# Weight sums for Winograd products made by accumulating DMAs, and six more pairs that use them

## The chip, the cores and the metric

The kernel runs on one core of a Trainium2 chip. The metric is the device time of one execution in microseconds, as the median of several runs. The engines are called as the profile calls them: PE (TensorE, matrix multiplications), PEld (its weight loads), DVE (VectorE, elementwise), ACT (ScalarE, activations and casts), POOL (GpSimd, here almost only an issuer of DMAs) and SP (SyncE, an issuer of DMAs). All DMAs run on the core's 16 DMA engines.

## The reference

Two layers, 256 positions, width 2048, float32. Layer 0 mixes with a gated MLP, layer 1 with latent attention, and each is followed by a convolutional feed-forward part. The change concerns the mixer of layer 0:

```python
def gmlp_mixer(x, w_in, ln_g, ln_b, w_s, b_s, w_out):
    z = jax.nn.gelu(x @ w_in)                  # w_in: 2048 x 12288
    u, v = jnp.split(z, 2, axis=-1)
    v = layer_norm(v, ln_g, ln_b)
    ...
    s = jnp.einsum('gij,bnjgd->bnigd', w, v) + ...
    return (u * s.reshape(B, S, GM_HALF)) @ w_out      # w_out: 6144 x 2048
```

`x @ w_in` is called the input projection here (first its V half, then its U half), the last line the output projection, also called spatial projection.

## The kernel before, in words

**Products.** The operands are float32. Each is split into a high part that TensorE takes in its faster float32 form and a low rest; a product of blocks is then three matmuls, high by high, low by high and high by low, each with 512 columns. The weights come in pieces of 1 MB, a "pair": two blocks of 128 rows (k) by 1024 columns, that is four quarters of 128 x 512. With the two halves of the 256 positions, a pair takes eight block products, 24 matmuls ("wide", `Banks.eight`). A "seven" pair (`Banks.seven`) uses Winograd's form of the 2 x 2 product: seven block products, 21 matmuls, for which sums of the quarters of the weights are needed, and sums and differences of the activations.

**Feed.** `Feed` streams the pairs in the order of use. `_load` issues the DMA of a pair from SP into one of three `raw` buffers. `_split` makes the parts: ACT casts the high part (`wh`, line 125), DVE subtracts for the low part (`wl`, line 128). For a seven pair `_seven` first makes the sums on DVE (`ts`, line 135: one addition of 1024 columns and two of 512), and casts and subtracts them too (`th`, `tl`). These parts lie in 14 buffers with the tag `big`, which are also used by activations. `next` runs two splits and two more loads ahead of use. In the feed-forward parts some pairs are "parked": made ahead in idle time, stored in DRAM and fetched by POOL; that stays as it is.

**Stages.** The V half of the input projection has six groups of eight pairs (until about 255 us), the U half six groups (until about 535 us), the output projection two halves of 24 pairs, in the order of the table `PLAN`: a number is the pair of k blocks, the letter its kind (e wide, s seven, p parked). The activations of a pair are made by `Acts.make`, in another form for a seven pair.

**Rows for the norm.** In the U half each group normalizes a part of v on DVE (`norm_v`, lines 831 and 832) with rows that POOL fetches by DMA (`row_v`, line 808, tiles `vr`). The first of these fetches stands right after the V half; the matmuls of `spatial` need the normalized v, and they stand third in the first U group.

**Order.** Each engine executes its instructions in the order of the program. An instruction that waits for a semaphore holds up all behind it on its engine. POOL and SP too: a DMA that waits stands in front of those behind it. `behind` places a DMA's issue in that order behind the latest matmul; it makes no wait.

Of the kernel before, what the change touches and what calls it, by code (L numbers as in the profile page):

```python
# [66 lines left out]
KEEP = {"wide": 4, "seven": 6, "parked": 6}  # L69


def plan(n_k):
# [4 lines left out]
class Feed:  # L77
# [3 lines left out]
    def __init__(self, nc, pin, behind, order, pool, dram, chunks):  # L81
        self.pin, self.behind, self.order, self.sums = pin, behind, order, None
        self.nc, self.pool, self.dram, self.chunks = nc, pool, dram, chunks
        self.kept = {}
        self.raw, self.parts = {}, {}
        self.loaded = self.split = self.used = 0

    def _load(self):
        ap, cols, kind = self.chunks[self.loaded][:3]
        if kind == "parked":  # L90
            self.fetch(self.loaded)
            self.loaded += 1
            return
        t = self.pool.tile([P, 2048], F32, tag="raw", name=f"raw{self.loaded}", bufs=SLOTS["raw"])
        if len(ap.shape) == 3:
            self.behind(self.nc.sync.dma_start(t.rearrange("p (k c) -> p k c", k=ap.shape[1]), ap))
        else:
            step = 1024 if self.loaded < 3 else cols
            for o in range(0, cols, step):
                self.behind(self.nc.sync.dma_start(t[:, o : o + step], ap[:, o : o + step]))  # L100
        self.raw[self.loaded] = t
        self.loaded += 1

    def _split(self):
        i = self.split
        cols, kind = self.chunks[i][1:3]
        if kind == "parked":
            self.split += 1
# [12 lines left out]
        self.parts[i] = (hi, lo)  # L121
        self.split += 1
# [8 lines left out]
    def _seven(self, i, raw):  # L131
# [78 lines left out]
def trunk(ctx: ExitStack, tc: tile.TileContext, x, xT, gm_in, gm_wout, ffn_up, ffn_dn,  # L210
# [30 lines left out]
            order(ins, recent[0])  # L241


    chunks, parked = [], []
    n_up = ffn_up.shape[1]
    for g in range(6):
        for p in V_PAIRS[g]:
# [7 lines left out]
    def back(w, n_k):  # L255

        for hf, units in enumerate(plan(n_k)):
            c = slice(hf * 1024, (hf + 1) * 1024)
            for u, kind in units:
                if 2 * u + 1 == n_k:  # L260
                    chunks.append((w[2 * u, :, c], 1024, kind))
                    continue
                if kind == "parked":
                    parked.append(len(chunks))
                chunks.append((w[2 * u : 2 * u + 2, :, c].rearrange("k p c -> p k c"), 2048, kind))

    back(gm_wout, NF_GM)
# [137 lines left out]
    class Banks:  # L405
# [29 lines left out]
        def seven(self, a, sums, wh, wl, th, tl, turned=0, across=False):  # L435
# [4 lines left out]
            self.to("q4", a[1][1], th, tl, 1536)  # L440
            self.to("q5", s1, th, tl, turned)
            self.to("p7", s3, th, tl, 512 - turned)
            self.to("p6", s2, th, tl, 1024)

        def rest(self):

# [46 lines left out]
    def down(n_k, src, tag, ln, acts, skew=SKEW, tiles=None, beside=None):  # L493
# [6 lines left out]
        for hf, units in enumerate(seq):  # L500
# [3 lines left out]
            for i, (u, kind) in enumerate(units):  # L504
# [13 lines left out]
                elif kind == "wide":  # L518
                    acc.eight(a, *got)
                else:  # L520
                    acc.seven(a, sums, *got, 512 if kind == "parked" else 0)
# [229 lines left out]
    for gi in range(6):  # L751
# [600 lines left out]
```

## Time and profile before

| | us |
|---|---|
| time, median of 3 runs (2465.39 to 2465.87) | 2465.41 |
| the profiled execution, first to last instruction | 2464.6 |
| PE busy in it | 2458.1 |
| DVE busy | 2054.7 |
| ACT busy | 1459.3 |
| POOL busy | 104.2 |
| share of the time in which the DMA engines move weights for SP's queue | 52.9% |
| the same for POOL's queue | 15.8% |

A matmul's duration in the profile is its passage through the array; the next one starts before it ends, so a stage's pace is read from its busy time over its number of matmuls. Times within the span count from its start. In the views, "[1.76 <-DMA vr<-gbrows]" behind an instruction is the time that its engine sat idle before it, and what ended that; "x40, 1024.0 KB, 4.8" behind a DMA are its count, its size and the median time in us from its issue to its landing.

### The profile page before, as it was taken

How to read it: one execution, taken by the hardware profiler on the slowest of the kernel's cores; microseconds unless marked ns; L12 is line 12 of the kernel's file. 1: busy time of each engine (PE TensorE's matmuls, PEld its weight loads, DVE VectorE, ACT ScalarE, POOL GpSimd, SP SyncE). 2: the span in 40 equal slices, each digit the busy share in tenths (PEclk: the TensorE clock that was granted, in tenths of full speed). 3: DMA queues.
4: the chain of work that ended last, by engine and by line, in shares of the span. 5: the costliest groups of instructions: out<-in, count | busy, mean ns of one | idle time of the engine just before them, and what ended most of it. 6: DMA issues, size and time to landing. Idle time of an engine off the chain costs nothing. (4 is left out here: it accounts for less than half of the span.)

```text
span 2464.6 us, 32483 instructions
## 1 busy us (share of the span) xinstructions
PE 2458.1 (100%) x12494; PEld 2091.3 (85%) x12494; DVE 2054.7 (83%) x2734; ACT 1459.3 (59%) x1967; POOL 104.2 (4%) x202
## 2 busy tenths in 40 slices
PE   9999999999999999999999999999999999999999
PEld 7888888888888888888888888988888888888887
DVE  7999999989897788778777997867598787878798
ACT  6666665566565666656554566665565665555453
POOL 0000000000000000000001000000000000000000
PEclk9999999999999999999999999999999999999999
DMA  7555666656665778778868885544478787777885
GB/s 291 202 208 205 226 204 202 205 188 205 222 212 198 241 282 314 300 279 300 322 218 318 301 301 182 184 170 156 172 269 309 275 305 304 295 265 278 299 324 201
DMA packets 116428, 611.94 MB, mean 248 GB/s; under 512 B 10648, under 2 KB 10912, under 8 KB 75184
## 3 DMA queue, kind: packets, MB, share of 16 engines
q1 hardware_dynamic: 90128, 462.47, 52.9%
q0 software_dynamic: 26144, 147.39, 15.8%
q8 instruction: 98, 1.61, 0.3%
q14 instruction: 58, 0.48, 0.1%
HBM read 544.75 MB, written 65.06 MB: 247 GB/s over the span
## 5 line engine op out<-in xcount | busy, mean ns | idle before, releaser
L128 DVE TENSOR_TENSOR wl<-raw,wh 128x1024 fp32r<-128x1024 f32 (+4 forms) x645 | 958.4, 1501 | 169.5 <-ACT wh L125 124.0
L125 ACT CAST wh<-raw 128x1024 fp32r<-128x1024 f32 (+4 forms) x645 | 809.0, 1278 | 356.8 <-PE up L230 80.7
L230 PE MATMUL up<-xhl,wh 128*128 128x512 f32 x2624 | 611.4, 390 | 0.0
L230 PEld LDWEIGHTS up<-xhl,wh 128*128 128x128 f32 x2624 | 487.4, 188 | 97.8
L230 PEld LDWEIGHTS up<-xhl,wl 128*128 128x128 f32 x2624 | 325.8, 192 | 6.4
L230 PE MATMUL up<-xhl,wl 128*128 128x256 f32 x2624 | 328.1, 283 | 0.0
L125 ACT CAST th<-ts 128x1536 fp32r<-128x1536 f32 (+1 forms) x138 | 142.5, 1052 | 110.9 <-DVE ts L135 80.3
L230 PE MATMUL ub<-wh,xhl 128*128 128x512 f32 x576 | 179.5, 393 | 0.0
L128 DVE TENSOR_TENSOR tl<-ts,th 128x1536 fp32r<-128x1536 f32 (+1 forms) x138 | 163.2, 1221 | 10.4 <-PE dn_p L230 3.4
L230 PEld LDWEIGHTS ub<-wh,xhl 128*128 128x128 f32 x576 | 108.1, 188 | 24.2 <-issue 1.9
L230 PE MATMUL ub<-wl,xhl 128*128 128x512 f32 x288 | 112.1, 389 | 0.0
L135 DVE TENSOR_TENSOR ts<-ts,raw 128x512 f32<-128x512 f32 x138 | 95.1, 689 | 1.4
L135 DVE TENSOR_TENSOR ts<-raw 128x1024 f32<-128x1024 f32 x69 | 84.3, 1221 | 6.1 <-PE ub L230 3.8
L230 PE MATMUL mo<-wh,oT 128*128 128x512 f32 x256 | 82.5, 401 | 0.0
L230 PE MATMUL v_q<-wh,xhl 128*128 128x512 f32 x224 | 70.7, 391 | 0.3 <-ACT wh L125 0.3
L230 PEld LDWEIGHTS ub<-wl,xhl 128*128 128x128 f32 x288 | 54.1, 188 | 11.3
L230 PE MATMUL v_p<-wh,xhl 128*128 128x512 f32 x192 | 59.9, 389 | 0.0
L230 PEld LDWEIGHTS mo<-wh,oT 128*128 128x128 f32 x256 | 45.5, 189 | 7.1
L230 PEld LDWEIGHTS v_q<-wh,xhl 128*128 128x128 f32 x224 | 42.0, 188 | 10.5 <-ACT wh L125 1.9
L230 PE MATMUL mo<-wl,oT 128*128 128x512 f32 x128 | 50.1, 391 | 0.0
L724 ACT ACTIVATE lny<-lnt,lncol 128x128 f32<-128x128 f32 x96 | 36.6, 472 | 15.6 <-PE lnt L720 15.5
L388 DVE TENSOR_TENSOR h_0a<-up,lo_0a 128x256 f32<-128x256 f32 x41 | 17.2, 421 | 33.0 <-ACT lo_0a L386 33.0
(1838 smaller groups left out, 4338.4 us busy)
## 6 DMA issues: line engine op xcount, KB each, us to landing
raw<-in_ffn_up_dram SPq DMA_DIRECT2D x172, 1024.0 KB, 7.0
raw<-in_gm_in_dram SPq DMA_DIRECT2D x93, 1024.0 KB, 5.3
raw<-in_ffn_dn_dram SPq DMA_DIRECT2D x68, 1024.0 KB, 7.2
raw<-in_gm_wout_dram SPq DMA_DIRECT2D x48, 1024.0 KB, 5.3
praw<-in_ffn_dn_dram POOLq DMA_DIRECT2D x16, 1024.0 KB, 13.9
keptth<-pth POOLq DMA_DIRECT2D x16, 1024.0 KB, 8.1
kepttl<-ptl POOLq DMA_DIRECT2D x16, 1024.0 KB, 8.8
fth<-keptth POOLq DMA_DIRECT2D x16, 1024.0 KB, 9.4
```

Of the source, the lines that this page charges most:

```text
L125: cast = self.nc.scalar.copy(hi, raw)
L128: self.nc.vector.tensor_tensor(lo, raw, hi.bitcast(F32), ALU.subtract)
L135: add = lambda o, a, b: self.nc.vector.tensor_tensor(o, a, b, ALU.add)
L230: recent[0] = nc.tensor.matmul(o, l, r, start=start, stop=stop, skip_group_check=True)
L388: nc.vector.tensor_tensor(h, acc[:, 0:S], lo, ALU.add)
L724: nc.scalar.activation(y[:, j], t[:, j * P : (j + 1) * P], AF.Identity, bias=lncol[:, o : o + 1], scale=lncol[:, g : g + 1])
```

## The change

A new kind of pair, "t" (summed), is added. Its four sums aren't made on DVE from the raw quarters, but ahead of time in DRAM, by `give`: POOL issues a DMA that writes the first quarter r0 four times into a DRAM buffer `given` (r0 r0 r0 r0), and three accumulating DMAs that add r1 to the first three, r2 to the last three, and r3 to the third. Source and target both lie in DRAM. `sums_ahead` takes the fourteen pairs two at a time, one step of both at each call, and is called after every second pair of V groups 1 to 5 (20 steps) and of the U groups until it is through (8 more). In the output projection a summed pair is loaded by three DMAs of SP: the quarters r1, r2, r3 into `raw` (r0 isn't used alone), and the sums into a `big` buffer. The table for the output projection has 14 "t" and 5 "s" pairs, where there were 13 "s"; the program has 18 matmuls fewer.

```diff
-PLAN = {NF_GM: ("0e 1e 2s 3e 4e 5s 6e 7e 8s 9e 10e 11s 12e 13e 14s 15e 16e 17s 18e 19e 20s 21e 22e 23e",
-                "23e 22e 21e 20s 19e 18e 17s 16e 15e 14s 13e 12e 11s 10e 9e 8s 7e 6e 5s 4e 3e 2e 1e 0e"),
+PLAN = {NF_GM: ("0e 1e 2s 3e 4t 5e 6e 7t 8e 9e 10t 11e 12t 13e 14t 15e 16t 17e 18t 19e 20s 21e 22e 23e",
+                "23e 22e 21e 20s 19e 18t 17e 16t 15e 14t 13e 12t 11e 10t 9e 8s 7t 6e 5s 4t 3e 2e 1e 0e"),
...
-KINDS = {"e": "wide", "s": "seven", "p": "parked"}
+KINDS = {"e": "wide", "s": "seven", "p": "parked", "t": "summed"}
...
 def _load(self):
...
-        if len(ap.shape) == 3:
+        if kind == "summed":
+            d = self.given.pop(self.loaded)
+            s = self.pool.tile([P, 2048], F32, tag="big", name=f"ts{self.loaded}", bufs=SLOTS["big"])
+            self.behind(self.nc.sync.dma_start(t[:, 512:1024], ap[:, 0, 512:1024]))
+            self.behind(self.nc.sync.dma_start(t[:, 1024:2048], ap[:, 1]))
+            self.behind(self.nc.sync.dma_start(s, d))
+            t = (t, s)
+        elif len(ap.shape) == 3:
...
 def _split(self):
...
+        if kind == "summed":
+            big = lambda n: self.pool.tile([P, 2048], F32R, tag="big", name=f"{n}{i}", bufs=SLOTS["big"])
+            wh, wl, th, tl = [big(n) for n in ("wh", "wl", "th", "tl")]
+            self._cast(wh[:, 0:1536], wl[:, 0:1536], raw[0][:, 512:2048])
+            self._cast(th, tl, raw[1])
+            self.parts[i] = (wh, wl, th, tl)
+            self.split += 1
+            return
...
+    def give(self, i):
+
+        ap, pin = self.chunks[i][0], self.pin
+        d = self.dram.tile([P, 2048], F32, tag=f"given{i}", name=f"given{i}", bufs=1)
+        self.given[i] = d
+        o = d.rearrange("p (n c) -> p n c", n=4)
+        r = lambda k, f, n: ap[:, k : k + 1, f * 512 : f * 512 + 512].to_broadcast([P, n, 512])
+        for n, (t, x) in enumerate(((o, r(0, 0, 4)), (o[:, 0:3], r(0, 1, 3)), (o[:, 1:4], r(1, 0, 3)), (o[:, 2:3], r(1, 1, 1)))):
+            ins = self.nc.gpsimd.dma_start(t, x) if n == 0 else self.nc.gpsimd.dma_start(t, x, accum_op=ALU.add)
+            self.behind(pin(ins))
+            yield
...
+    def sums_ahead():
+
+        for i, j in zip(summed[::2], summed[1::2]):
+            for _ in zip(feed.give(i), feed.give(j)):
+                yield
+
+    ahead = sums_ahead()
...
             got = feed.next()
+            if gi and c % 2:
+                next(ahead, None)
...
             got = feed.next()
+            if c % 2:
+                next(ahead, None)
```

How this stands in POOL's order, first at the start of the V groups. `wT` are the spatial weights, a `given` number is one pair's buffer, DMASW counters count landings of POOL's own DMAs. Before, the row fetches (`vr`) follow the last of `wT`:

```order
L781 DMA wT_1978<-in_w_sT_dram 128x256 [waits DMAHW6_49,PE_49]
L782 MEMSET wT_1969 64x2x64 [waits DMASW0_49,Pool_49]
L782 MEMSET wT_1972 64x2x64 [waits DMASW2_49]
L782 MEMSET wT_1975 64x2x64 [waits DMASW3_49]
L782 MEMSET wT_1978 64x2x64 [waits DMASW4_49]
L808 DMA vr_1998<-gbrows 128x512 [waits DMASW1_49,DVE_49,Activation_49]
L808 DMA vr_2000<-gbrows 128x512 [waits DVE_49,Activation_49]
```

Now the first two pairs follow there:

```order
L171 DMA given_526<-in_gm_wout_dram 512x1x512
L171 DMA given_528<-in_gm_wout_dram 512x1x512
L822 MEMSET wT_2022 64x2x64 [waits DMASW2_49]
L822 MEMSET wT_2025 64x2x64 [waits DMASW3_49]
L822 MEMSET wT_2028 64x2x64 [waits DMASW4_49]
L171 DMA given_526<-in_gm_wout_dram 128x3x512 [waits DMASW5_49]
L171 DMA given_528<-in_gm_wout_dram 128x3x512 [waits DMASW6_49]
L171 DMA given_526<-in_gm_wout_dram 128x3x512 [waits DMASW7_49,DMASW1_49]
L171 DMA given_528<-in_gm_wout_dram 128x3x512 [waits DMASW0_49]
L171 DMA given_526<-in_gm_wout_dram 128x512 [waits DMASW1_49]
L171 DMA given_528<-in_gm_wout_dram 128x512 [waits DMASW2_49]
```

Forty such DMAs, ten pairs, stand ahead of the first row fetch, and none waits for another engine. The end of that series, and what follows it:

```order
L171 DMA given_1779<-in_gm_wout_dram 128x3x512 [waits DMASW7_49]
L171 DMA given_1781<-in_gm_wout_dram 128x3x512 [waits DMASW0_49]
L171 DMA given_1779<-in_gm_wout_dram 128x512 [waits DMASW3_49,DMASW1_49]
L171 DMA given_1781<-in_gm_wout_dram 128x512 [waits DMASW4_49,DMASW2_49]
L848 DMA vr_2048<-gbrows 128x512 [waits DVE_49,Activation_49]
L848 DMA vr_2050<-gbrows 128x512 [waits DVE_49,Activation_49]
```

The row fetches of the first U group are now behind the last accumulating steps of the fifth two pairs; the sixth and the seventh two pairs stand ahead of the fetches for the third and the fourth part of v. The compute engines' order in the whole input projection is as it was.

In SP's order at the start of the output projection, before:

```order
L96 DMA raw_3945<-in_gm_wout_dram 128x2x1024 [waits DMAHW7_49,DVE_49]
L96 DMA raw_3999<-in_gm_wout_dram 128x2x1024 [waits DMAHW0_49,DVE_49]
L96 DMA raw_4032<-in_gm_wout_dram 128x2x1024 [waits DMAHW1_49,DVE_49,Activation_49]
L96 DMA raw_4064<-in_gm_wout_dram 128x2x1024 [waits DMAHW2_49,DVE_49]
L96 DMA raw_4131<-in_gm_wout_dram 128x2x1024 [waits DMAHW3_49,DVE_49]
```

and now:

```order
L103 DMA raw_4015<-in_gm_wout_dram 128x2x1024 [waits DMAHW7_49,DVE_49]
L98 DMA raw_4069<-in_gm_wout_dram 128x512 [waits DMAHW0_49,DVE_49]
L99 DMA raw_4069<-in_gm_wout_dram 128x1024
L100 DMA ts_4070<-given_526 128x2048 [waits DMASW5_49,DMASW3_49,DMASW7_49,DMASW1_49,PE_49]
L103 DMA raw_4105<-in_gm_wout_dram 128x2x1024 [waits DMAHW1_49,DVE_49,Activation_49]
```

A load of one pair has become three, and the third waits for TensorE (PE), which frees the buffer, and for the chain of that pair, ahead of the next raw load.

More of the change, by code (lines that the diff above doesn't have):

```diff
@@ L56 @@
 SLOTS = {"big": 14, "raw": 3, "side": 6}
-PLAN = {NF_GM: ("0e 1e 2s 3e 4e 5s 6e 7e 8s 9e 10e 11s 12e 13e 14s 15e 16e 17s 18e 19e 20s 21e 22e 23e",
-                "23e 22e 21e 20s 19e 18e 17s 16e 15e 14s 13e 12e 11s 10e 9e 8s 7e 6e 5s 4e 3e 2e 1e 0e"),
+PLAN = {NF_GM: ("0e 1e 2s 3e 4t 5e 6e 7t 8e 9e 10t 11e 12t 13e 14t 15e 16t 17e 18t 19e 20s 21e 22e 23e",
+                "23e 22e 21e 20s 19e 18t 17e 16t 15e 14t 13e 12t 11e 10t 9e 8s 7t 6e 5s 4t 3e 2e 1e 0e"),
         NF_FF: ("0e 1p 2e 3s 4e 5e 6p 7e 8s 9e 10e 11p 12e 13s 14e 15p 16e 17s 18e 19s 20e 21e",
                 "21e 20e 19p 18e 17s 16e 15p 14e 13s 12e 11p 10s 9e 8s 7p 6e 5s 4e 3e 2e 1e 0e")}
-KINDS = {"e": "wide", "s": "seven", "p": "parked"}
+KINDS = {"e": "wide", "s": "seven", "p": "parked", "t": "summed"}
 FIRST = ((19, 1), (20, 0), (20, 2))
 LEAD = 5
-KEEP = {"wide": 4, "seven": 6, "parked": 6}
+KEEP = {"wide": 4, "seven": 6, "parked": 6, "summed": 6}
 def plan(n_k):
@@ L83, in __init__ @@
         self.nc, self.pool, self.dram, self.chunks = nc, pool, dram, chunks
-        self.kept = {}
+        self.kept, self.given = {}, {}
         self.raw, self.parts = {}, {}
@@ L241, in behind @@
             order(ins, recent[0])
-    chunks, parked = [], []
+    chunks, parked, summed = [], [], []
     n_up = ffn_up.shape[1]
@@ L264, in back @@
                     parked.append(len(chunks))
+                if kind == "summed":
+                    summed.append(len(chunks))
                 chunks.append((w[2 * u : 2 * u + 2, :, c].rearrange("k p c -> p k c"), 2048, kind))
@@ L433, in first, with seven @@
             self.begun.update(DIRECT)
-        def seven(self, a, sums, wh, wl, th, tl, turned=0, across=False):
+        def seven(self, a, sums, wh, wl, th, tl, turned=0, across=False, at=(1536, 1024)):
             s1, s2, s3, s4 = sums
@@ L439, in seven @@
             self.to("p1", a[0][0], wh, wl, 512 if across else 0)
[L440 removed]
+            q4, p6 = at
+            self.to("q4", a[1][1], th, tl, q4)
             self.to("q5", s1, th, tl, turned)
[L442 to L443 removed]
+            self.to("p7", s3, th, tl, 512 - turned if p6 == 1024 else 1536)
+            self.to("p6", s2, th, tl, p6)
         def rest(self):
@@ L520, in down @@
                 else:
-                    acc.seven(a, sums, *got, 512 if kind == "parked" else 0)
+                    acc.seven(a, sums, *got, 512 if kind == "parked" else 0, at=(1024, 512) if kind == "summed" else (1536, 1024))
                     if u == last:
```

## The prediction

> **What bounds the kernel now.** I read the page first: the busy shares say which engine sets the end.
>
> ```profile
> span 2464.6 us, 32483 instructions
> PE 2458.1 (100%) x12494; PEld 2091.3 (85%) x12494; DVE 2054.7 (83%) x2734; ACT 1459.3 (59%) x1967; POOL 104.2 (4%) x202
> ```
>
> TensorE (PE) is never idle, so a matmul that goes is time that goes, and any wait that reaches TensorE is time that comes. The next view is the table of windows, cut where the change works: V part of the input projection from the first possible sum to the first row fetch (57.5 to 253.8 us), the first two groups of its U part, and the output projection (columns: stretch; then busy us and instructions of PE, PEld, DVE, ACT, POOL; clock; share of the 16 DMA engines; GB/s).
>
> ```profile
> 57.50:253.80 196.30, 196.30 (x868) 162.54 (x867) 189.39 (x170) 129.62 (x149) 0.23 (x2) 1.00 0.59 208
> 253.80:302.70 48.90, 48.90 (x214) 39.89 (x213) 44.31 (x58) 29.31 (x40) 4.29 (x9) 1.00 0.68 230
> 302.70:346.90 44.20, 44.20 (x198) 35.50 (x197) 42.83 (x44) 27.20 (x28) 2.12 (x4) 1.00 0.64 211
> 535.00:789.80 254.80, 254.80 (x1137) 211.16 (x1137) 227.76 (x255) 147.65 (x145) 0.72 (x1) 1.00 0.63 211
> ```
>
> Three readings. TensorE starts a matmul every 196.30 / 868 = 0.226 us. VectorE (DVE) is busy 189.39 of 196.30 us in V, 96%, so it can hardly catch up there after a delay. The DMA engines are 59% to 68% busy, always with weights; GpSimd (POOL) has almost nothing to do until 253.8 us. What it does then is in its timeline:
>
> ```profile
> 253.83 0.54 POOL L808 DMA_DIRECT2D vr<-gbrows  x1 [195.98 <-issue]
> 269.55 0.54 POOL L808 DMA_DIRECT2D vr<-gbrows  x1 [2.46 <-DVE vrs L351]
> 302.68 0.54 POOL L808 DMA_DIRECT2D vr<-gbrows  x1 [32.59 <-DVE u0u L453]
> 306.87 1.74 POOL L808 DMA_DIRECT2D vr<-gbrows  x3 [3.65 <-DVE v L896]
> 346.93 0.54 POOL L808 DMA_DIRECT2D vr<-gbrows  x1 [38.32 <-DVE u1u L453]
> ```
>
> It fetches the rows (vr) of the gating unit's norm. The timelines of VectorE and TensorE show who waits for them:
>
> ```profile
> 260.86 0.75 DVE L831 SCALAR_TENSOR_TENSOR v<-v,vmv,vr 128x512 f32<-128x512 f32 x1 [1.76 <-DMA vr<-gbrows]
> 279.87 2.35 DVE L128 TENSOR_TENSOR tl<-ts,th 128x1536 fp32r<-128x1536 f32 x2
> 282.39 0.62 PE L230 MATMUL ub<-th,xhl 128*128 128x512 f32 x2
> ```
>
> VectorE already waits 1.76 us for the first row, and at 282.39 TensorE begins on weights whose low part VectorE finishes at 282.2. There is no reserve at this place: what the rows come late, TensorE waits.
>
> **The change, part by part.** *Matmuls.* Thirteen pairs with 21 products of halves become nineteen (five "s" and fourteen "t" in the new plan; the words of the change say 17). Six pairs lose three matmuls each: 18 x 0.226 = 4.1 us less. This is the whole gain, 0.17% of the time.
>
> *VectorE in the output projection.* Eight pairs fewer are summed there. By the groups of that window, kept apart by shape:
>
> ```profile
> L135 DVE TENSOR_TENSOR ts<-raw 128x1024 f32<-128x1024 f32 x12 | 14.7, 1222 | 4.0 <-PE ub L230 3.4 <-PE wo_q L230 0.7
> L135 DVE TENSOR_TENSOR ts<-ts,raw 128x512 f32<-128x512 f32 x25 | 17.2, 687 | 0.2
> L128 DVE TENSOR_TENSOR tl<-ts,th 128x1536 fp32r<-128x1536 f32 x13 | 22.8, 1753 | 0.2 <-ACT th L125 0.2
> L128 DVE TENSOR_TENSOR wl<-raw,wh 128x2048 fp32r<-128x2048 f32 x33 | 75.4, 2288 | 14.6 <-ACT wh L125 12.0 <-issue 2.1
> ```
>
> That removes 8 x (1.22 + 2 x 0.69) = 20.8 us. Against it stand six pairs more whose sums are split, 6 x (1.75 + 2.29 - 2.29) = 10.5 us (the second split of 2048 columns takes what two of 1536 and 512 took, within 0.15 us), and six left operands made in the seven-product form, with one more 512-column operation of 0.69 us and four small ones each, an estimated 2 us. VectorE's load there stays at 227.76 of 254.80 us within a few us, so this is costed at nothing; TensorE hides it, and with that cover gone it would be those few us. SyncE's loads there grow by 14 x 0.79 MB = 11 MB on 211 GB/s x 254.8 us = 54 MB, a DMA share of 0.63 that goes to 0.76. A fetched sum waits for one of 14 buffers that TensorE frees, with the next raw load behind it in SyncE's queue; the buffer is one that TensorE read four or five pairs before the sum's own pair, 20 us and more by 21 to 24 matmuls of 0.226 us, against a landing of
>
> ```profile
> raw<-in_gm_wout_dram SPq DMA_DIRECT2D x48, 1024.0 KB, 5.3
> ```
>
> and the split after it. I take 0, at most one landing, 5 us, and no gain.
>
> *The sums themselves.* Per pair the chain writes 1.05 + 0.79 + 0.79 + 0.26 = 2.88 MB, the first a copy, the other 1.84 MB accumulating. The order shows that GpSimd issues forty of these DMAs, for ten pairs, before the first row fetch, with nothing to hold them back but the step before. So they start at about 57.5 us and must be out by 253.8: 28.8 MB (10.5 copied, 18.4 accumulated) beside the loads. What the loads take and what all engines can move:
>
> ```profile
> q1 hardware_dynamic: 6072, 40.71, 59.1%
> raw<-in_gm_in_dram SPq DMA_DIRECT2D x40, 1024.0 KB, 4.8
> 2168.00:2188.00 20.00, 20.00 (x119) 17.84 (x119) 14.03 (x23) 11.64 (x20) 1.00 (x2) 1.00 1.04 414
> 1876.00:1926.00 50.00, 50.00 (x287) 44.18 (x286) 43.71 (x60) 31.23 (x44) 3.97 (x7) 1.00 0.94 351
> q0 software_dynamic: 720, 4.73, 59.3%
> q1 hardware_dynamic: 478, 3.52, 44.0%
> raw<-in_ffn_up_dram SPq DMA_DIRECT2D x4, 1024.0 KB, 9.7
> ```
>
> The first two rows are the queues of 57.5 to 253.8 us (packets, MB, share of 16 engines; then the median landing); the next two are the fullest stretches I found, 414 GB/s for 20 us and 351 for 50; the last three belong to 2168 to 2188 us. There GpSimd's queue took more than SyncE's, and a weight load landed in 9.7 us instead of 4.8. So the chain will not stand back behind the loads.
>
> No accumulating DMA is in this trace. From below it costs what a copy costs (it can't be cheaper, and it adds bytes, so a gain is excluded); an upper end isn't there, but two copies are the nearest price, since it must read what stands in the buffer as well as what is added. With c GB/s for all engines the work to be done by the first row fetch takes (40.8 + 10.5 + 18.4 a) MB / c, a = 1 or 2, against 196.3 us:
> a = 1: 168 us at 414, 199 us at 351: 28 us early to 2 us late.
> a = 2: 213 us at 414, 251 us at 351: 16 to 55 us late.
> I take a = 2 and 382 GB/s, halfway: 230 us, **34 us late**. All of it reaches TensorE, at the first row fetch, or sooner where a load that lands 5 us later starves VectorE; the sum of bytes is the same.
>
> The Trainium skill, page "DMA: Bandwidth & Descriptors", section "SDMA does more than copy", lists the add as an elementwise reduce of two streams, which speaks for a = 2; no run here shows it yet. The same page ("Where 436 GB/s comes from") holds that HBM binds a core at about 358 GB/s; by it the lateness would be 246 - 196 = 50 us. The row with 414 GB/s speaks against it for 20 us, the row with 351 for it over 50.
>
> *Two more rounds*, of two pairs each, 2.1 MB copied and 3.7 accumulated, stand between row fetches. The sixth, from 269.55 to 302.68: loads 230 GB/s x 33.1 us = 7.6 MB, and 9.4 MB with a = 2, 17.0 / 0.382 = 45 us, 11.5 us late. The row that waits behind it landed (minimum, median, maximum) in
>
> ```profile
> DMA to landing us min/median/max: 3.4/4.2/7.1
> 312.83 1.41 DVE L831 SCALAR_TENSOR_TENSOR v<-v,vmv,vr 128x512 f32<-128x512 f32 x2
> 357.08 1.42 DVE L831 SCALAR_TENSOR_TENSOR v<-v,vmv,vr 128x512 f32<-128x512 f32 x2
> ```
>
> so it was there at 302.68 + 4.2 = 306.9 and read at 312.83, 6 us of slack: 5.5 us late. The seventh, from 306.87 + 1.74 = 308.6 to 346.93: 8.1 + 9.4 = 17.5 MB, 46 us for 38.3, 7.6 us late with 6.0 of slack (346.93 + 4.2 to 357.08): 1.6 us. Together 7 us; with a = 1 the two rounds need 35 and 36 us, and both late ends lie within the slack: 0. At 351 GB/s and a = 2 they come to 15 us.
>
> **The sum** on the profiled execution: 2464.6 - 4.1 + 34 + 7 = 2501.5 us. The median of the timed runs, 2465.4, is 0.8 above that span: 2502 us, 1.5% slower. The bounds with a = 2 go from 2465 - 4 + 16 + 2 = 2479 to 2465 - 4 + 55 + 15 = 2531.
>
> **The rivals.**
> *The chain is cheap* (the other side: not slower). An accumulating packet moves as fast as a copied one, a is up to about 1.5 at 414 GB/s, (51.3 + 27.5) / 0.414 = 190 us, the chain is out before 253.8 us and hides under the loads. Then only the matmuls count: 2465.4 - 4.1 = 2461.3. It decides at 9.8 us per step of two DMAs (196.3 us / 20). For it: POOL idle for 196 us, 41% of the engines free, and TensorE unhurt in the fullest stretch. Against it: in that stretch VectorE had 6 of 20 us free, in V it has 7 of 196.
> *The chain is slow*: each accumulating step waits for the landing of the one before, and a is 3 or more, or the steps don't overlap. At a = 3 and 382 GB/s: (51.3 + 55.1) / 0.382 = 278 us, 82 us late, and the two rounds, each 3.7 / 0.382 = 9.6 us longer, add 7 + 19 = 26: 2465.4 - 4.1 + 82 + 26 = 2569 us; more beyond. For it: nothing in this trace has such a chain. Against: two pairs are interleaved, so that one moves while the other lands.
> *The output projection stalls*: SyncE, blocked on a buffer for a fetched sum, holds up the raw loads. Priced above at up to 5 us: 2466 if the chain is cheap. Alone it leaves the time within what can't be told from no change.
> *A gain beyond the 18 matmuls* would need idle TensorE time that the page doesn't have.
>
> **How the numbers follow.** A difference under 0.2%, 4.9 us, is what these runs can't tell from no change: the cheap chain falls there, since 4.1 us is less. Forecast (chain 10 to 70 us late): 0.52. Slow chain: 0.15. Cheap chain, with or without a small stall: 0.29. More than 0.2% faster: 0.04. So slower 0.67, same 0.29, faster 0.04. The likeliest case's own range is 2479 to 2531; the range given reaches to the cheap chain below and to a = 3 above: 2460.5 to 2570.
>
> **What would show it.** Right: in the changed profile GpSimd issues the first vr clearly after 253.8 us, VectorE's wait for DMA vr grows from 1.76 us to tens, TensorE has idle time ended by VectorE near 255 to 320 us, the DMA share of V is near 1, raw<-in_gm_in lands in 7 us and more, and the output projection takes 4 us less than its 254.8. Wrong: the first vr still at 254 us, TensorE without a gap; then an accumulated MB is no dearer than about 1.5 copied ones. If TensorE stalls before 250 us and vr is in time, the bytes were right and the place wrong: the loads paid. Stalls between 535 and 790 us would show the buffers of the fetched sums as the price.

## The result, and the profile after

| | before | after |
|---|---|---|
| time, median (lowest to highest), us | 2465.40 (2465.39 to 2465.87) | 2546.42 (2544.71 to 2548.25) |
| ratio to before, 95% interval | | 1.0327 (1.0314 to 1.0340) |
| the profiled execution, us | 2464.6 | 2546.4 |

The change costs 81 us; the forecast was 37. The page of the changed kernel, its first lines, and the granted clock in 40 slices:

```profile
span 2546.4 us, 32605 instructions
PE 2473.1 (97%) x12476; PEld 2094.4 (82%) x12476; DVE 2055.7 (81%) x2738; ACT 1468.0 (58%) x1971; POOL 161.5 (6%) x258
PEclk9999789999999999999999999999999999999999
```

TensorE was 100% busy and now is 97%. Its clock was at 0.9 or more in all slices before; now the fifth and the sixth slice, 255 to 382 us, stand at 0.7 and 0.8. The table of windows, as in the prediction (stretch; busy us and instructions of PE, PEld, DVE, ACT, POOL; clock; DMA share; GB/s), says where:

```profile
57.50:100.00 42.50, 41.65 (x183) 33.88 (x182) 35.18 (x32) 21.38 (x18) 5.17 (x5) 1.00 1.02 284
150.00:200.00 50.00, 45.63 (x190) 37.22 (x189) 41.77 (x38) 29.49 (x36) 8.18 (x8) 0.93 1.03 283
250.00:300.00 50.00, 36.37 (x150) 28.88 (x148) 24.16 (x27) 19.51 (x27) 8.46 (x9) 0.88 1.05 270
300.00:350.00 50.00, 23.77 (x89) 18.16 (x90) 31.10 (x40) 14.97 (x17) 11.30 (x16) 0.68 0.86 205
400.00:450.00 50.00, 41.06 (x167) 31.30 (x166) 37.53 (x39) 26.45 (x29) 6.32 (x8) 0.93 0.91 245
```

From the first sum to 300 us the DMA engines are full (1.02 to 1.05 in these windows, where V had 0.59), at only 270 to 284 GB/s. GpSimd's timeline shows when the chain is through:

```profile
309.64 0.81 POOL L171 DMA_DIRECT2D given<-in_gm_wout_dram  x1 [4.06 <-DMA given<-in_gm_wout_dram]
310.19 3.00 POOL L848 DMA_DIRECT2D vr<-gbrows  x5
```

and VectorE's, who had waited for it:

```profile
314.95 0.75 DVE L871 SCALAR_TENSOR_TENSOR v<-v,vmv,vr 128x512 f32<-128x512 f32 x1 [34.08 <-DMA vr<-gbrows]
```

The first row is fetched at 310.2 instead of 253.8 us, 56 us late, and VectorE's wait for it grew from 1.76 to 34 us. TensorE's waits up to 900 us (who waits for whom; us in all, times, longest; six rows of fifteen):

```profile
PE ub L257 <- DVE v L872: 31.2, 1, 31.2
PE ub L257 <- DVE v L828: 8.7, 1, 8.7
PE v_p L257 <- DVE v3u L481: 4.4, 1, 4.4
PE ub L257 <- DVE wl L143: 4.3, 4, 1.7
...
PE lnt L750 <- DVE res L709: 2.0, 1, 2.0
...
PE upf L257 <- ACT xhl L757: 1.8, 1, 1.8
```

All its rows but the one for the warm-up at the start, which stood there before too, sum to 67.6 us.

To see where the loss arises in this kernel and in the experiments, I took the start of every matmul in two traces, counted from the last one, and subtracted. A kernel with fewer matmuls has a constant ahead of the output projection that only counts these (-4.1 us with 18 fewer, -3.1 with 12, as the kernels without sums show); it is taken off. What is left is how late TensorE is at four places, in us:

| kernel | end of V | behind the first rows (300) | end of U (540) | behind the output projection (800) |
|---|---|---|---|---|
| the change | 12.2 | 57.8 | 80.1 | 86.4 |
| plain_steps | 9.3 | 16.0 | 25.0 | 31.2 |
| no_chain | 0 | 0 | 0.3 | 6.3 |
| two_rounds | 2.9 | 3.1 | 3.1 | 10.0 |
| three_ahead | 6.6 | 8.2 | 51.9 | 57.7 |
| rows_on_sync | 11.1 | 33.3 | 57.0 | 63.8 |
| late_rows | -0.6 | 47.0 | 48.5 | 54.8 |
| eight_no_chain | 0 | 0 | 0 | 0 |
| eight_burst | 19.7 | 27.5 | 27.5 | 27.5 |
| eight_paced | 13.0 | 20.2 | 46.2 | 46.2 |
| eight_single | 0.5 | 7.1 | 25.9 | 25.9 |
| eight_cheap | -0.2 | 4.5 | 4.5 | 4.5 |
| eight_clear | -0.3 | 0.8 | 1.5 | 1.4 |

So the change loses 80 us in the input projection, 6 at the end of the output projection, and gains the 4.1 of the 18 matmuls: 82.

### The profile page after: what moved, and what is told of

It is laid out like the page before. It is cut to its first block, busy times and chain, and to the rows that moved or that the text cites. A ratio compares the mean times of both kernels' runs of the same rounds, so it can differ in the third digit from the quotient of the medians.

```text
span 2546.4 us, 32605 instructions
## 1 busy us (share of the span) xinstructions
PE 2473.1 (97%) x12476; PEld 2094.4 (82%) x12476; DVE 2055.7 (81%) x2738; ACT 1468.0 (58%) x1971; POOL 161.5 (6%) x258
## 3 DMA queue, kind: packets, MB, share of 16 engines
q0 software_dynamic: 43168, 187.76, 23.6%
## 5 line engine op out<-in xcount | busy, mean ns | idle before, releaser
L140 ACT CAST th<-ts 128x1536 fp32r<-128x1536 f32 (+2 forms) x136 | 152.3, 1139 | 104.6 <-DVE ts L150 83.5
L143 DVE TENSOR_TENSOR tl<-ts,th 128x1536 fp32r<-128x1536 f32 (+2 forms) x136 | 176.1, 1327 | 14.7 <-ACT th L140 9.0
L150 DVE TENSOR_TENSOR ts<-raw 128x1024 f32<-128x1024 f32 x61 | 74.3, 1219 | 21.9 <-DMA raw<-in_gm_in_dram 21.3
L150 DVE TENSOR_TENSOR ts<-ts,raw 128x512 f32<-128x512 f32 x122 | 83.6, 685 | 1.3
L171 POOL DMA_DIRECT2D given<-in_gm_wout_dram x56 | 57.4, 1077 | 303.5 <-DMA given<-in_gm_wout_dram 303.4
L257 PE MATMUL ub<-v,wT 128*128 128x512 f32 (+1 forms) x64 | 24.5, 537 | 31.2 <-DVE v L872 31.2
L871 DVE SCALAR_TENSOR_TENSOR v<-v,vmv,vr 128x512 f32<-128x512 f32 x24 | 17.4, 744 | 44.5 <-DMA vr<-gbrows 44.5
L257 PEld LDWEIGHTS v_q<-wh,xhl 128*128 128x128 f32 x224 | 42.3, 189 | 10.5 <-ACT wh L140 1.9
```

Source lines behind the costliest of these rows:

```text
L140: cast = self.nc.scalar.copy(hi, raw)
L143: self.nc.vector.tensor_tensor(lo, raw, hi.bitcast(F32), ALU.subtract)
L150: add = lambda o, a, b: self.nc.vector.tensor_tensor(o, a, b, ALU.add)
L171: ins = self.nc.gpsimd.dma_start(t, x) if n == 0 else self.nc.gpsimd.dma_start(t, x, accum_op=ALU.add)
L257: recent[0] = nc.tensor.matmul(o, l, r, start=start, stop=stop, skip_group_check=True)
L871: nc.vector.scalar_tensor_tensor(t, t, mv[b][:, 0:1], rows[0], ALU.subtract, ALU.mult)
```

## Experiments

My theory after this look: the chain's bytes cost about twice their copies in engine time, that time is not there in V, and the rows wait for it; the 6 us behind the output projection belong to the new table of pairs. The rivals: the queue, not the bytes; the place of the rows; the loads that land late.

### Without the add, without the chain, with part of it

**plain_steps** (all four steps are copies):

```diff
-            ins = self.nc.gpsimd.dma_start(t, x) if n == 0 else self.nc.gpsimd.dma_start(t, x, accum_op=ALU.add)
+            ins = self.nc.gpsimd.dma_start(t, x)
```

> The changed kernel with its 56 DMAs between DRAM buffers as plain copies, no addition (the sums are left out; bytes written, steps, waits and order stay). Theory (the add is the price: an accumulated MB takes all 16 engines about 6.6 us in the changed kernel's profile, a copied one 2.6): the V part's chain needs 28.8 MB x 2.6 = 76 us of engine time, is out before the first row fetch, the row fetch is on time, and a few us of late weight loads remain: 2467 to 2478 us. Rival (the chain's shape is the price: dependent steps, landings, short rows, whatever the operation): no better than 2530 us.

Measured: 2495.01 us, ratio 1.0121 (1.0104 to 1.0138). Between the two: the add is 51 of the 81 us, but the same bytes merely copied still cost 30. The DMA queues from 57.5 us to about the first row fetch, first of the change (to 310 us), then of plain_steps (to 268 us); columns: packets, MB, share of the 16 engines, and for an issue its count, KB and median landing:

```profile
q0 software_dynamic: 11981, 28.44, 57.9%
q1 hardware_dynamic: 6672, 42.99, 44.6%
raw<-in_gm_in_dram SPq DMA_DIRECT2D x40, 1024.0 KB, 10.0
```

```profile
q1 hardware_dynamic: 6097, 40.79, 52.8%
q0 software_dynamic: 7649, 28.71, 44.0%
raw<-in_gm_in_dram SPq DMA_DIRECT2D x39, 1024.0 KB, 9.2
```

A MB copied from DRAM to DRAM takes 0.440 x 210.5 / 28.71 = 3.2 us of all engines, a MB of weights 0.528 x 210.5 / 40.79 = 2.7. In the change GpSimd's queue takes 0.579 x 252.5 = 146 us, of which 10.5 MB copied are 34; the other 17.95 MB, accumulated, take 112 us, 6.3 us per MB. That is twice a copy, as assumed. But the prediction priced a copy by the rate of the loads, 382 GB/s, 2.6 us per MB.

**no_chain** and **two_rounds** (the sums of all fourteen pairs, or of all but the first four, are left out and their second load is the weights themselves):

```diff
-            d = self.given.pop(self.loaded)
+            d = None
...
-    ahead = sums_ahead()
+    ahead = iter(())
```

```diff
-        for i, j in zip(summed[::2], summed[1::2]):
+        for i, j in zip(summed[:4:2], summed[1:4:2]):
```

> The changed kernel without any DMA between DRAM buffers: the fourteen pairs load the weights themselves where the sums would be (the sums are left out); the output projection keeps its plan, loads and matmuls. Theory (18 matmuls less, and the 5.7 us lost behind the output projection belong to its own new plan, whose last pairs leave VectorE no lead): 2465.4 - 4.1 + 5.7 = 2467 us. Rival (that loss is an after-effect of the stalls before): 2461.3 us.

> The changed kernel with the sums of the first four pairs only (the other ten load unsummed weights; their sums are left out). Theory (engine time): the two rounds end near 165 us, TensorE loses by then the 3.6 us it had lost at that place in the changed kernel, and no row is late: the time of the kernel without a chain + 4, 2465 to 2472 us. Rival (any accumulating chain upsets the V part, however short): 10 us or more above the kernel without a chain.

Measured: 2468.58 us, ratio 1.0012 (1.0002 to 1.0021), and 2469.96, ratio 1.0018 (1.0009 to 1.0027). Without any sum the new table is no gain: its 4.1 us are there until 783 us of no_chain, and 6.3 are lost right behind. TensorE's waits in no_chain, apart from the warm-up and one of 0.3 us, and the last windows of its output projection and of the boundary behind it:

```profile
PE lnt L750 <- DVE res L709: 2.0, 1, 2.0
PE upf L257 <- ACT xhl L757: 1.7, 1, 1.7
```

```profile
730.00:780.00 50.00, 50.00 (x222) 41.41 (x221) 48.73 (x54) 33.43 (x32) 0.00 (x0) 1.00 0.71 243
780.00:800.00 20.00, 16.39 (x69) 13.09 (x68) 13.21 (x25) 11.21 (x26) 0.00 (x0) 0.83 0.34 134
```

VectorE is busy 48.7 of the last 50 us, so TensorE catches up with it, waits 3.7 us, and the clock of the next 20 us is 0.83. By the table two rounds of sums in V cost 3 us more; the medians of no_chain and two_rounds differ by 1.4.

**three_ahead** (three rounds in V, the other four between the row fetches of U):

```diff
-            if gi and c % 2:
+            if gi in (1, 2, 3) and c % 2:
                 next(ahead, None)
```

> The changed kernel with three rounds instead of five ahead of the first row fetch, the other four between the row fetches of the U groups. All sums are made. Theory (bytes: engine time lost at one place comes back at another): the first row is on time, but each of the four rounds in U costs what rounds six and seven cost, 11 us: 2461 + 6 + 7 + 45 = 2519 us. Rival (the order of GpSimd's queue alone: a row fetch stuck behind the chain): with three rounds out in time the loss is mostly gone, 2475 to 2485 us.

Measured: 2524.00 us, ratio 1.0234 (1.0219 to 1.0249). The bytes, then, more than the queue: three rounds cost 6.6 us in V, and the four others, with the rows only just behind each, 43.7 in U.

### The rows

**late_rows** makes the rows late without the bytes (no_chain with 25 small copies in a row ahead of the row fetches):

```diff
+LATE = 25
...
+    for i in range(LATE):
+        d = dram.tile([24, 512], F32, tag=f"late{i}", name=f"late{i}", bufs=1)
+        hop = tc.keep_in_program_order(nc.gpsimd.dma_start(d, gbd))
+        tc.add_manual_dep(hop.ins, recent[0].ins.name, mybir.DependencyInfo(
+            mybir.DependencyClass.Sync, mybir.DependencyReason.DATA), reason="late")
+        gbd = d
     rows0 = [row_v(0, 0), row_v(0, 1)]
```

> no_chain (its table, without the sums; the boundary's 6 us in it), with one thing added: 25 copies of the 48 KB of the row vectors from DRAM buffer to DRAM buffer, each waiting for the one before, from the last matmul of V on; the rows of U are fetched from the last copy. So the rows come some 50 to 70 us late, as in the change (56), with 2.4 MB of traffic in place of the chain's 46. Theory (at the start of U the change lost what the rows were late beyond some 20 us of cover, and the lower clock behind the wait): with the first row fetch at 302 to 320 us, 50 to 66 us late, TensorE loses 30 to 46 us, the granted clock of 300 to 350 us falls below 0.8, and the time is 2468.6 + 30 to 50 = 2499 to 2519. Rival (the lost time and the low clock come from the crowded DMA engines and late weights): under 2490, the clock near 1.

Measured: 2517.00 us, ratio 1.0209 (1.0193 to 1.0225). Its first row fetch on GpSimd, its one long wait of TensorE ("issue" where the view shows no releaser; the matmul behind it is the first that needs the normalized v), and two windows:

```profile
324.26 2.71 POOL L849 DMA_DIRECT2D vr<-late  x5 [2.02 <-DMA late<-late]
```

```profile
286.13 0.63 PE L258 MATMUL ub<-th,xhl 128*128 128x512 f32 x2
330.58 5.63 PE L258 MATMUL ub<-v,wT 128*128 128x512 f32 x12 [43.82 <-issue]
```

```profile
300.00:350.00 50.00, 17.95 (x65) 12.83 (x66) 20.52 (x25) 10.34 (x11) 9.73 (x19) 0.66 0.25 73
330.50:334.40 3.90, 3.82 (x5) 1.78 (x6) 3.90 (x7) 0.72 (x2) 1.08 (x2) 0.50 0.60 179
```

Rows 70 us late cost 47 us up to the second place of the table and 48.5 in all of U: 43.8 in this wait, 2.2 in three short ones, and some 2 at half clock, which the second window shows behind the wait. The DMA engines were a quarter busy. So late rows stop TensorE, and the clock falls at an idle TensorE, crowded engines or not. But the 23 us of lateness that were covered here can't be carried over to the change: in late_rows the matmuls on the normalized v stand behind those of the "th" weights, 65 matmuls later in TensorE's order than in the change, and the norm stands later in VectorE's order.

The change has the order of before at this place, and shows the cover itself. The first matmul on the normalized v in TensorE's timeline, before and then in the change:

```profile
271.42 1.24 PE L230 MATMUL ub<-v,wT 128*128 128x512 f32 x3
```

```profile
326.23 2.05 PE L257 MATMUL ub<-v,wT 128*128 128x512 f32 x2 [31.18 <-DVE v L872]
```

It stood 17.6 us behind the first row fetch and now stands 16.0 behind it. So 54.8 of the rows' 56.4 us reach TensorE, and half clock behind the wait makes them the 57.8 of the table. When TensorE came to this wait it was 23.6 us late already, by weights that came late: 12.2 us in V, the rest at the passage to U (the wait of 8.7 us for v L828, and low clock). By this trace that lateness isn't added to the rows'; it only leaves less of theirs to wait for. No run has the change's loads on time with its rows as late and its order kept, so this is read from the trace and not tested.

The Trainium skill, page "TensorE: Matmul & The Clock Gate", Part 1, says that an idle window of about 3.4 us puts the array back to half clock, and that it takes as long a busy one to come back. The 3.9 us at half clock behind the wait of late_rows agree with the way back; but in eight_cheap below a wait of 2.8 us, shorter than that window, was enough for half clock. The prediction had no such term.

**rows_on_sync** takes the rows out of the chain's queue:

```diff
-            nc.gpsimd.dma_start(t, gbd[12 * i + 2 * g + f : 12 * i + 2 * g + f + 1, :].to_broadcast([P, 512]))
+            nc.sync.dma_start(t, gbd[12 * i + 2 * g + f : 12 * i + 2 * g + f + 1, :].to_broadcast([P, 512]))
```

> The change as it is, all seven rounds, but the row fetches of U are issued on SyncE's queue among the weight loads, so that nothing waits behind the chain but the chain itself. Theory (half of the loss is the place in the queue: three_ahead, with the rows ahead of four of the rounds, lost 52 us in V and U where the change lost 80; the rest is the engines' time, which seven full rounds take from the loads wherever the rows stand): 2505 to 2525. Rival (the queue alone: with the rows out of it only V's 12 us and the boundary's 6 stay): 2480 to 2485. Second rival (SyncE, which now waits for row buffers too, delays the weight loads by as much): 2540 or more.

Measured: 2523.26 us, ratio 1.0232 (1.0218 to 1.0246). The queue was worth 23 us, not the loss. 46 us are still lost in U, and the first row fetch is itself late on the new queue, in SyncE's timeline:

```profile
273.08 4.59 SPq L848 DMA_DIRECT2D vr<-gbrows  x4
```

The landings between 57.5 and 310 us (count, KB, median us):

```profile
raw<-in_gm_in_dram SPq DMA_DIRECT2D x42, 1024.0 KB, 10.0
vr<-gbrows SPq DMA_DIRECT2D x8, 256.0 KB, 13.1
```

Weights land in 10.0 us instead of 4.8 and rows in 13.1 instead of 4.2: in full engines everybody is late.

### Where the price of a burst comes from

For the next kernels I made a table with 9 "s" and 8 "t" pairs, with VectorE's work at the end of the second half relieved:

```diff
-PLAN = {NF_GM: ("0e 1e 2s 3e 4t 5e 6e 7t 8e 9e 10t 11e 12t 13e 14t 15e 16t 17e 18t 19e 20s 21e 22e 23e",
-                "23e 22e 21e 20s 19e 18t 17e 16t 15e 14t 13e 12t 11e 10t 9e 8s 7t 6e 5s 4t 3e 2e 1e 0e"),
+PLAN = {NF_GM: ("0e 1e 2s 3e 4e 5s 6e 7t 8e 9s 10e 11t 12e 13s 14e 15t 16e 17t 18e 19e 20s 21e 22e 23e",
+                "23e 22e 21e 20s 19e 18t 17e 16s 15e 14t 13e 12t 11e 10s 9e 8t 7e 6s 5e 4e 3e 2e 1e 0e"),
```

**eight_no_chain** has it without sums:

> Leaves the sums out (the summed pairs' second load comes from the weights themselves), and has a new table of pairs: still 17 seven-product pairs, but 9 's' and 8 't', the last of them six pairs before the end ('... 10s 9e 8t 7e 6s 5e 4e 3e 2e 1e 0e' in the second half) where the changed kernel's were '... 8s 7t 6e 5s 4t 3e 2e 1e 0e'. Theory (the 6 us that every kernel with the new table has lost by 800 us, behind the output projection, come from VectorE, whose lead over TensorE has gone from 8-11 us to about zero with the two 's' and two 't' pairs at the end): the 4.1 us of the 18 matmuls stay and the 6 us go, 2465.4 - 4.1 = 2461.3 us, 2460.5 to 2463. Rival (the 6 us come with summed pairs as such, their three loads or their buffers): 2465 to 2468.6, little better than no_chain's 2468.6.

Measured: 2462.88 us, ratio 0.9990 (0.9981 to 0.9999). My expectation miscounted: the change has 19 seven-product pairs (as the prediction says), this table 17. So it saves 12 matmuls, 2.7 us, and not 4.1; 2465.3 - 2.7 = 2462.6 is within 0.3 us of what was measured. The 6 us are gone:

```profile
730.00:780.00 50.00, 50.00 (x222) 41.40 (x221) 44.30 (x43) 29.45 (x28) 0.00 (x0) 1.00 0.75 268
780.00:800.00 20.00, 20.00 (x100) 16.28 (x99) 14.99 (x24) 15.09 (x35) 0.00 (x0) 1.00 0.17 54
```

VectorE has 5.7 of the last 50 us free, and TensorE waits for nobody. That its load at the end is the cause fits both runs; the table differs at other places too, so it isn't isolated.

**eight_burst** makes this table's sums as the change does, four rounds; **eight_paced** lets each of these steps wait for a matmul as well, half of them in V, half in U:

```diff
             self.behind(pin(ins))
+            self.after_pe(ins)
             yield
...
+    feed.after_pe = lambda ins: tc.add_manual_dep(ins.ins, recent[0].ins.name, mybir.DependencyInfo(
+        mybir.DependencyClass.Sync, mybir.DependencyReason.DATA), reason="pace")
...
-            if gi and c % 2:
+            if gi and (c == 5 or c == 1 and gi % 2):
...
-            if c % 2:
+            if c == 4 or c == 7 and g in (0, 2):
```

> As eight_paced, the same table and the same four rounds, but issued as in the change: each step as soon as the one before has landed, from 55 us on. Theory (engine time): at 50 to 55 us a round the fourth ends at about 265 us, some 10 us behind the place of the first row fetch; V loses about 10 us to the full engines (3.1 with two rounds, 6.6 with three) and the rows up to 10 more: 2471 to 2482. Rival (what counts is only the total of bytes, 4/7 of the change's): 2461.3 + 80 x 4/7 = 2507. If pacing does nothing, it equals eight_paced.

> The whole computation: the table with 9 's' and 8 't', and the sums made by accumulating DMAs as in the change, but four rounds instead of seven, and each step also waits for the matmul that was recorded last where it stands, with eight steps in V (one per 20 to 40 us) and eight in U behind the row fetches. Theory (what costs is engine time beyond what the loads leave free, not the accumulating DMA as such): eight pairs need 8 x (1.05 MB x 2.6 to 3.2 + 1.84 MB x 6.6) = 120 to 124 us of all 16 DMA engines, of which V and U leave some 81 + 86 us free by the shares of before; half in each, the share reaches about 0.9 and nobody waits long: 2461.3 to 2465, that is up to 4 us faster than before. Rival (any accumulating transfer slows the weight loads it runs beside, wherever it stands): two rounds cost two_rounds 3.1 us in V, so four cost 6 to 10: 2467 to 2472.

Measured: eight_burst 2490.00 us, ratio 1.0100 (1.0086 to 1.0113); eight_paced 2507.89, ratio 1.0168 (1.0155 to 1.0182). Here my theory fell. Spread over twice the time, the same bytes cost 18 us more, with engine time to spare (V's share 0.70 to 0.94), and even the rival's 2472 was too low. What eight_paced does to the loads around one step of V (162 to 175 us):

```profile
raw<-in_gm_in_dram SPq DMA_DIRECT2D x3, 1024.0 KB, 11.9
given<-in_gm_wout_dram POOLq DMA_DIRECT2D x2, 1024.0 KB, 11.9
```

A step is two transfers at once, and the weight loads in flight share the engines with them: 11.9 us to land instead of 4.8. The Trainium skill, page "DMA: Bandwidth & Descriptors", section "Queues, rings and completion order", says that each engine takes turns between the queues that have work, packet by packet; the shares of the change above, 57.9% and 44.6%, are near each other, as that would give; no run here shows the turns themselves. VectorE, which waits for the load, can't make it up with 3% to 4% of free time in V, so each step leaves its few us for good. The new theory: it isn't the bytes that count, nor the mean share, but how far one burst delays a load beyond its lead.

**eight_single** halves the burst: one pair per step, 10 steps in V, 21 in U (at other weight pairs than in eight_paced).

```diff
-            for _ in zip(feed.give(i), feed.give(j)):
-                yield
+            steps = (feed.give(i), feed.give(j))
+            for n in range(8):
+                next(steps[n % 2])
+                yield
...
-            if gi and c % 2:
+            if gi and c in (2, 6):
...
-            if c % 2:
+            if c in (0, 4, 6) or c == 7 and g < 4:
```

> The whole computation, with eight_paced's table and its waits for a matmul, but every step is one transfer of one pair instead of two pairs' at once, so that a burst is half as large: 10 steps in V, 21 in U (and one behind them). In eight_paced each double step raised a weight load's landing from about 5 to 9-14 us, and VectorE, which has 1.5 of 50 us free in V, never made the wait up: 2 to 5 us lost per step, 46 in all. Theory (the loads are issued some 10 us before their first use; a burst costs what it delays a load beyond that): a step of 0.79 MB accumulated takes 0.79 x 6.6 = 5.2 us of all engines, a load lands in 5 + 5 = 10 us, little is lost: 2463 to 2475. Rival (what is lost goes with the accumulated bytes, not with the size of a burst): as eight_paced, 2500 to 2510.

Measured: 2492.30 us, ratio 1.0116 (1.0097 to 1.0135). In V the theory holds: ten transfers cost 0.5 us, where eight_paced's sixteen cost 13 and ten in proportion would cost 8. In V the loads land in

```profile
raw<-in_gm_in_dram SPq DMA_DIRECT2D x40, 1024.0 KB, 7.5
```

U lost 25 us all the same. There two steps at the end of a group followed each other some 5 us apart, a double burst again, and the row fetches stand in the same queue; this run doesn't tell the two apart.

**eight_cheap** has smaller transfers. A pair's sums are made with 1.05 MB accumulated instead of 1.84, in six steps, and the steps have other places: none in U beside the first row fetch of a group, and twelve in the output projection:

```diff
+        q = lambda n: o[:, n : n + 1]
+        r = lambda k, f, n=1: ap[:, k : k + 1, f * 512 : f * 512 + 512].to_broadcast([P, n, 512])
+        for step in ([(o[:, 0:4:3], r(0, 0, 2), 0)], [(q(0), r(0, 1), 1), (q(3), r(1, 0), 1)],
+                     [(q(1), q(0), 0)], [(q(1), r(1, 0), 1)], [(q(2), q(1), 0)], [(q(2), r(1, 1), 1)]):
+            for t, x, add in step:
+                ins = self.nc.gpsimd.dma_start(t, x, accum_op=ALU.add) if add else self.nc.gpsimd.dma_start(t, x)
...
+STEPS = {8 * g + c for g in range(1, 6) for c in (1, 3, 5, 7)}
+STEPS |= {48 + 8 * g + c for g in range(6) for c in ((4, 6, 7) if g < 4 else (4, 6))} | set(range(96, 120, 2))
```

> The whole computation, with the table of 9 's' and 8 't'. The sums of a pair are made with less accumulation, 1.05 MB instead of 1.84: a copy of r0 into the first and last quarter; r1 added to the first and r2 to the last; the first quarter copied to the second and r2 added; the second copied to the third and r3 added. That is six steps of one pair each, of at most 0.52 MB accumulated (0.52 x 6.6 = 3.5 us of all DMA engines), and they are spread over V (20 steps, one per second weight pair), U (16, none beside the first row fetch of a group) and the first half of the output projection (12), each behind a matmul. Theory (a burst costs what it delays a weight load, or a row, beyond the lead of some 5 us that it has): a load lands in 5 + 3.5 = 8.5 us, nothing is lost, and the time is that of eight_no_chain, 2462.9, to 2 us more: 2462.5 to 2465, that is 0 to 3 us faster than before. Rival (what is lost goes with the accumulated bytes: eight_single lost 26.5 us with 14.7 MB of them, here 8.4): 2462.9 + 15 = 2478. Second rival (the rows of U wait behind the steps on GpSimd's queue whatever their size: eight_single lost nearly all in U, 25 of 26 us): 2475 to 2485 with the loss in U, though V and the output projection lose nothing.

Measured: 2467.30 us, ratio 1.0007 (0.9998 to 1.0016). That a step stands ahead of row fetches in GpSimd's queue is no price of its own: with twelve steps of U so placed, U lost nothing behind its first group, nor did V or the output projection. By the accumulated bytes alone the time would have been 2478, as the expectation worked out. But the size of a transfer, the bytes in all and the places were changed together, so which of them saved U isn't isolated. The whole loss, 4.5 us, lies at the passage from V to U, one wait of TensorE and the clock behind it:

```profile
PE ub L265 <- DVE v L838: 2.8, 1, 2.8
```

```profile
250.00:300.00 50.00, 47.20 (x198) 37.99 (x197) 44.44 (x57) 30.71 (x40) 5.90 (x12) 0.97 0.73 227
257.70:261.00 3.30, 3.30 (x9) 2.55 (x9) 3.30 (x5) 3.30 (x11) 2.15 (x4) 0.50 0.93 293
```

**eight_clear** moves the two steps at that place to the last group of U:

```diff
-STEPS = {8 * g + c for g in range(1, 6) for c in (1, 3, 5, 7)}
+STEPS = {8 * g + c for g in range(1, 6) for c in (1, 3, 5, 7)} - {45, 47} | {88, 90}
```

> As eight_cheap, the whole computation, with two of its 48 steps moved: the last two of V (at 240 and 250 us) go to the last group of U, which has no row fetches left. In eight_cheap all that was lost against eight_no_chain, 4.2 us, was lost between 250 and 290 us: the two weight loads beside these steps landed 2 us late, at the one place where a cast on ScalarE stands ahead of the activations of V's last group, and TensorE waited 2.8 us for VectorE and then ran with the lower clock. Theory: these 4 us go, 2462.9 to 2464.5, 1 to 2.5 us faster than before. Rival (the first step that stands in U's first group, or the rows' own traffic, costs the same): 2467, as eight_cheap.

Measured: 2464.61 us (2463.96 to 2465.82) beside 2465.87 (2465.19 to 2466.98), ratio 0.9995 (0.9986 to 1.0004). The sums of eight pairs, made whole, now cost 1.2 us more than leaving them out (1.3 under before, where eight_no_chain is 2.4 under its own), where eight_burst's cost 27. Its median is 1.3 us under before's, and the interval doesn't rule out that they are equal. TensorE's waits of the input and output projection:

```profile
PE ub L265 <- DVE v L838: 0.9, 1, 0.9
PE ub L265 <- DVE u0w L492: 0.3, 1, 0.3
```

## Why the prediction was right and wrong

The direction, the mechanism (a chain of sums too slow for V, rows late behind it) and the places announced held: the first row well after 253.8 us, VectorE's wait in the tens, V's DMA share at 1, loads landing in 10 us. The size was less than half, because three terms of the sum were too small: the chain's lateness (34 us, measured 56), the two rounds in U (7, measured 22.3) and the output projection (nothing, measured 6.3). By its steps:

- *Matmuls*, -4.1 us: right. The output projection, between the places where it began and ended at 535.0 and 789.8 us before, takes 4.0 us less than its 254.8:

```profile
615.10:865.90 250.80, 250.15 (x1112) 207.03 (x1110) 226.81 (x254) 155.36 (x144) 0.72 (x1) 1.00 0.74 259
```

- *VectorE in the output projection*, "costed at nothing": wrong by 6 us. Its load over the whole stretch is as priced, 226.81 us in this row beside 227.76; but the table puts two "s" and two "t" pairs close to the end, where VectorE has 1.3 of 50 us free (no_chain). The mean of the stretch hid its end; it should have been cut into pieces.
- *SyncE's buffers*, 0: right; TensorE has no wait between 540 and 860 us of the change.
- *The chain*, "a = 2 and 382 GB/s ... 34 us late": 56 us late. The factor was right (6.3 us per MB against 3.2 for a copy). The base was wrong: 382 GB/s, halfway between two full stretches of before, is what loads reach, and a copy from DRAM to DRAM takes 1.2 times as long as a load (3.2 to 2.7 us per MB in plain_steps). With the measured prices the work is 40.8 x 2.6 + 10.5 x 3.2 + 18.4 x 6.3 = 256 us against 196, 60 late. The Trainium skill, page "DMA: Bandwidth & Descriptors", section "Where 436 GB/s comes from", gives 358 GB/s as the bound of a core, by which the prediction had 50. The engines were full at 284 GB/s in the change and at 331 in plain_steps, so that bound wasn't what filled them in either.
- *"All of it reaches TensorE ... the sum of bytes is the same"*: right, by the trace of the change, but for 1.6 us. 54.8 of the 56.4 us reach the first matmul on the normalized v, and the 23.6 us that late loads had cost until there are part of them. The prediction read the place off the weights used at 282.39 us; the matmul that waited is the one of 271.42.
- *Two more rounds*, 7 us: 22.3. I counted the bytes of the loads and priced only the rows' slack; what the bursts of two pairs do to the landing of the weight loads beside them had no price. eight_paced lost 26 us in U to two such rounds. The change's own rounds were not run apart, so how its 22.3 divide between loads and rows stays open.
- *Missing*: the clock. The change lost 86.4 us before the gain, and TensorE's waits sum to 67.6. Some 13.6 of the other 18.8 are matmuls at half clock: the granted clock is 0.50 in six stretches behind or around these waits (the longest is 298 to 332 us), and TensorE is busy for 27 us in them. The remaining 5 us lie in neither; their cause stays open.

With what was measured at each place, clock included: -4.1 + 57.8 + 22.3 + 6.3 = 82.3 us, against 81.8 in the profiled executions.

Of the rivals, the cheap chain is out, as is a = 3. That TensorE stalls in V on late loads was named as a sign, with the rows in time; it did stall there, 12.2 us, but the rows came late too and took these in.

## What to carry to other kernels

In this kernel "the DMA engines are 59% busy" was room only for transfers short enough that the loads beside them still landed within their lead: two pairs at once, 0.5 to 2.1 MB a step, cost 18 us more when they were spread out than back to back, and steps of a quarter to half a MB, with fewer bytes accumulated, cost 1 to 5 us. Before giving an idle queue work, ask which latency on the busy one has no slack, and look at the last pieces of a stage, not at its mean. And add to every stall of TensorE some us for the clock behind it.

## What the hardware showed that I had not expected

- An accumulating DMA from DRAM to DRAM takes 6.3 us of all 16 engines per MB, a copy 3.2, a weight load 2.6 to 2.7 beside them (2.9 in before: 0.591 x 196.3 / 40.71).
- A wait of TensorE costs more than its length: 4.5 us for one of 2.8 at the passage from V to U (eight_cheap), 6.3 for two of 2.0 and 1.7 behind the output projection (no_chain). The granted clock stood at 0.50 behind them (257.7 to 261.0 us of eight_cheap), 0.83 in the mean of the 20 us window of no_chain.
- Pacing made it worse: the same four rounds cost 27.5 us back to back and 46.2 spread over V and U. Why continuous crowding costs less per byte than separate bursts was not measured by itself.
